# Down projection with an eighth ring slot, spaced ring loads and 35 new visits, and a last gate/up pair ordered product by product

## The chip, the cores and the metric

The kernel runs on one core of one Trainium2 chip. The core's engines work side by side, each on its own queue, in order: TensorE (PE) multiplies matrices and accumulates in PSUM; VectorE (DVE) and ScalarE (ACT) do elementwise work; GpSimd (POOL) does elementwise work and issues DMAs that accumulate; SyncE (SP) only issues DMAs. ACT issues DMAs too. An engine that waits for a semaphore holds up everything behind it on its queue. The metric is the device time of one execution in microseconds (us); less is better.

## The reference

One block of a hybrid model, in float32, for 512 tokens of width 2048. Only the last two steps matter here:

```python
D_FF = -((-8 * D_MODEL) // (3 * 256)) * 256        # 5632
...
    h = h + mixed @ w_out[l]
    v = rmsnorm(h, ffn_norm_w[l])
    h = h + (jax.nn.silu(v @ w_gate[l]) * (v @ w_up[l])) @ w_down[l]
return rmsnorm(h, final_norm_w)
```

Ahead of them stand a state-space mixer and a sparse attention; the change does not touch them.

## The kernel before

**Arithmetic.** Products keep float32 precision by splitting each operand into a high part (rounded to fp32r) and a low part (the rest); each product is three matmuls, high x high, high x low and low x high (L1252 to L1254, each with a moving operand of 256 columns). A 2 x 2 block product is done in Strassen's way with seven products M1 to M7 instead of eight. The tokens are split in two halves of 256 and the weights into quadrants "11", "12", "21", "22". The seven forms of the activations are made once ("V0", "VV", "T0" to "T3" for gate/up); the weight forms are made on the fly: "S1" is 21 + 22, "S3" is 21 + 11, and M6 and M3 take sums that DVE adds in place.

**Steps.** The feed-forward part is one list of steps (class `Step`, L1234). A step is one product over n rows (chunks of 128) of one weight block, 3 n matmuls. `run_step` (L1242) writes out, in order: `feed`, the step's `before`, `prep` of what lies two steps ahead, the matmuls (each chunk with a `tick` of the background tasks in `Sched`), and `after`, which takes the product out of PSUM. Each engine works through its own share of that list in order. `form` (L1205) makes the sums (DVE) and the high half (ACT); `prep` (L1221) makes the low half (DVE, L121) and frees the weight block. High halves are thus made up to three steps ahead and low halves up to two. They lie in R, 48 rows of 128 columns, which every step shares.

**Weight blocks.** `advance` (L1171) goes through the list `loads` in order and gives each block the free place that has been free longest: in Z (38 rows in the down projection, 48 before), E (8 rows), A[0:8] in gate/up, or A2 = A[70:76] in the down projection. Then it issues the load on SP; a block with `plus` gets an accumulating DMA on POOL on top; a block with `both` is the sum of two blocks, made by POOL.

**Gate/up.** 22 pairs u, each with two sides (0 gate, 1 up) of 7 products with n = 8: side 0 first, then side 1, in the order `SEQ`. A side has five blocks from DMA, two of them with an accumulating DMA. `gu_after` (L1419) combines the products in the tile CT, applies the norm and silu after side 0's M4 and multiplies the sides after side 1's M4. `g_forms` (L1457) then makes the seven forms of the result, spread over 14 ticks, in ST, and writes them to the DRAM tile g_d[u] (1.8 MB) on ACT's queue. A is one tile: HH is A[20:28], CT is A[28:44], ST is A[44:76], and the forms lie in A[44:72].

**Down projection.** The result is 8 column pairs j, each summed over the 22 chunks. It is done in 36 visits (j, n): visit v multiplies the next n chunks of column j, 7 products of 3 n matmuls, in the order `SEQ_D`. The accumulators H[j] lie in A[10 j : 10 j + 10] (H[7] in Z); `load_h` (L1555) puts the residual h into rows 1 to 4 of H[j] from DRAM, on ACT's queue. The activations come back through a ring of 7 slots, the places where the seven gate/up forms lay (chunks 0 to 6 of each; a form has 8). `feed` (L1541), at each step, issues at most one load, G[n], on ACT's queue, once the slot's last user lies at least two steps back; `done` holds the step after which a slot is free. In the last pair, slot i is free after the i-th product of side 1. `quad(..., s3_by_pool)` makes S3 with POOL in the first six visits and with an accumulating DMA behind them. `d_after` adds the products to H[j]; a column's last visit also runs `add_x` and `squares`. `d_end` ends the last visit, norms and writes out. `down_before` (L1695) loads H[v + 1] at product 1 of visit v and there makes A2 known.

## Time and profile before

| | us |
|---|---|
| runs of the kernel | 2313.32, 2312.17, 2308.17 (median 2312.17) |
| the profiled execution: its span, from the first to the last instruction | 2311.7 |
| PE busy in the span | 2196.5 (95%) |
| DVE busy | 1809.7 (78%) |
| ACT busy | 1091.2 (47%) |
| end of the last gate/up product | 1800.2 |
| last matmul of the down projection | 2294.1 |

A row of a group or timeline names the kernel's line, the engine, the operation, the tile written and the tiles read. In a wait row the arrow points to what ended the wait. A line can be that of a helper: L118 makes a high half, L121 a low half, L127 is an add. In the windows, "x" counts the instructions that begin or run in a window, and PEclk is the mean clock that PE was granted, where 1.00 is full. Tiles keep the name of the allocation: u, V and T are ring slots, A holds the accumulators and g's forms, Z and E hold weight blocks, R holds high and low halves.

### The profile page before, as it was taken

The numbers are of one execution on the slowest core, as the hardware profiler recorded it, in microseconds if no ns is written. First come the engines' busy times: TensorE is split into PE (matmuls) and PEld (weight loads), VectorE is DVE, ScalarE is ACT, GpSimd is POOL, SyncE is SP. The second block draws the span as 40 slices with busy tenths as digits, with TensorE's granted clock in tenths as the row PEclk, the third lists the DMA queues.
The fourth block names the chain that finished last, engine by engine and source line by source line (L and its number), as shares of the span: only waits on it lengthen the run. The fifth ranks groups of instructions, "written<-read, shape, count | busy, mean of one in ns | idle before, by whom it ended". The sixth has DMA issues, their size and how long they took to land. (4 is left out here: it accounts for less than half of the span.)

```text
span 2311.7 us, 39742 instructions
## 1 busy us (share of the span) xinstructions
PE 2196.5 (95%) x15376; PEld 2039.8 (88%) x15376; DVE 1809.7 (78%) x2921; ACT 1091.2 (47%) x1768; POOL 422.2 (18%) x435
## 2 busy tenths in 40 slices
PE   7999988989989989999999999999999698989997
PEld 5888877878878878999999999999999698989997
DVE  7799754768788857888888888888888697878786
ACT  4554433757676634544444444444444243333353
POOL 1011214132232134100000000000101121212122
PEclk9999989999999999999999999999999899999998
DMA  5222432221233366787878787887878857677776
GB/s 176 89 74 74 133 110 87 73 72 63 76 101 125 105 198 180 207 233 219 242 217 243 221 249 226 245 227 231 233 219 250 323 170 264 186 254 233 259 162 171
DMA packets 151469, 417.34 MB, mean 181 GB/s; under 512 B 16320, under 2 KB 21968, under 8 KB 151280
## 3 DMA queue, kind: packets, MB, share of 16 engines
q1 hardware_dynamic: 99264, 250.99, 31.5%
q0 software_dynamic: 25456, 76.78, 17.3%
q10 hardware_dynamic: 26560, 87.04, 10.5%
q8 instruction: 120, 1.97, 0.3%
q14 instruction: 69, 0.57, 0.1%
HBM read 353.67 MB, written 57.15 MB: 178 GB/s over the span
## 5 line engine op out<-in xcount | busy, mean ns | idle before, releaser
L118 ACT ACTIVATE R<-Z 128x1024 fp32r<-128x1024 f32 (+4 forms) x488 | 441.5, 922 | 573.0 <-DVE Z L127 320.6
L121 DVE TENSOR_TENSOR R<-Z,R 128x1024 fp32r<-128x1024 f32 (+4 forms) x381 | 392.3, 1035 | 28.5 <-ACT R L118 19.7
L241 PE MATMUL ps_g<-u,whi 128*128 128x512 f32 x720 | 301.1, 418 | 9.5 <-ACT whi L118 9.5
L242 PE MATMUL ps_g<-u,whi 128*128 128x512 f32 x720 | 284.3, 395 | 0.0
L243 PE MATMUL ps_g<-u,wlo 128*128 128x512 f32 x720 | 284.3, 397 | 0.0
L1252 PE MATMUL ps_g<-u,R 128*128 128x256 f32 (+1 forms) x834 | 250.5, 300 | 0.7 <-ACT R L118 0.7
L1253 PE MATMUL ps_g<-u,R 128*128 128x256 f32 (+1 forms) x834 | 249.7, 299 | 0.0
L1254 PE MATMUL ps_g<-u,R 128*128 128x256 f32 (+1 forms) x674 | 200.5, 298 | 0.1
L1252 PE MATMUL ps_t<-u,R 128*128 128x256 f32 x688 | 194.0, 282 | 0.0
L1253 PE MATMUL ps_t<-u,R 128*128 128x256 f32 x688 | 193.9, 282 | 0.0
L1252 PE MATMUL ps_s<-u,R 128*128 128x256 f32 x686 | 193.7, 282 | 0.0
L1253 PE MATMUL ps_s<-u,R 128*128 128x256 f32 x686 | 193.5, 282 | 0.0
L118 ACT ACTIVATE whi<-wraw 128x512 fp32r<-128x512 f32 x196 | 122.4, 626 | 145.2 <-PE ps_g L242 94.6
L121 DVE TENSOR_TENSOR wlo<-wraw,whi 128x512 fp32r<-128x512 f32 x196 | 145.9, 748 | 46.1 <-ACT whi L118 45.4
L241 PEld LDWEIGHTS ps_g<-u,whi 128*128 128x128 f32 x720 | 137.7, 191 | 33.1 <-ACT whi L118 11.4
L1252 PEld LDWEIGHTS ps_g<-u,R 128*128 128x128 f32 x834 | 158.3, 190 | 6.6 <-ACT R L118 0.9
L243 PEld LDWEIGHTS ps_g<-u,wlo 128*128 128x128 f32 x720 | 136.7, 190 | 30.7 <-DVE wlo L121 0.7
L1253 PEld LDWEIGHTS ps_g<-u,R 128*128 128x128 f32 x834 | 158.3, 190 | 5.9
L1254 PE MATMUL ps_s<-u,R 128*128 128x256 f32 x566 | 160.0, 283 | 0.6 <-DVE R L121 0.6
L242 PEld LDWEIGHTS ps_g<-u,whi 128*128 128x128 f32 x720 | 137.7, 191 | 19.7
L121 DVE TENSOR_TENSOR E<-Z,R 128x1024 fp32r<-128x1024 f32 x107 | 130.4, 1218 | 5.6 <-ACT R L118 5.6
L127 DVE TENSOR_TENSOR Z<-Z 128x1024 f32<-128x1024 f32 (+5 forms) x119 | 126.2, 1061 | 8.3 <-POOL Z L127 5.3
(449 smaller groups left out, 6464.3 us busy)
## 6 DMA issues: line engine op xcount, KB each, us to landing
Z<-in_w_gate SPq DMA_DIRECT2D x96, 512.0 KB, 5.3
Z<-in_w_up SPq DMA_DIRECT2D x94, 512.0 KB, 7.3
wraw<-in_w_in SPq DMA_DIRECT2D x164, 256.0 KB, 3.0
g_d<-A ACTq DMA_DIRECT2D x22, 1792.0 KB, 7.1
u<-g_d ACTq DMA_DIRECT2D x12, 1792.0 KB, 16.3
Z<-in_w_gate POOLq DMA_DIRECT2D x37, 512.0 KB, 7.4
Z<-in_w_up POOLq DMA_DIRECT2D x36, 512.0 KB, 5.6
Z<-in_w_down SPq DMA_DIRECT2D x52, 320.0 KB, 5.8
```

Source lines behind the costliest of these rows:

```text
L118: act.activation(dst, src, AF.Copy, scale=scale)
L121: eng.tensor_tensor(dst, src, f(hi), ALU.subtract)
L127: eng.tensor_tensor(o, a, b, ALU.add)
L241: pe.matmul(p, hi_t[i][:, j, :], ah, start=(k == 0), stop=False)
L242: pe.matmul(p, hi_t[i][:, j, :], al, start=False, stop=False)
L243: pe.matmul(p, lo_t[i][:, j, :], ah, start=False, stop=(k == u.nk - 1))
L1252: pe.matmul(q, h[:, k, :], ah, start=(k == 0), stop=False)
L1253: pe.matmul(q, h[:, k, :], al, start=False, stop=False)
L1254: pe.matmul(q, l[:, k, :], ah, start=False, stop=(k == s.blk.n - 1))
```

## The change

- The ring gets an eighth slot, made of chunk 7 of each of the seven forms. What goes there (G[7] and G[15]) is written to a DRAM tile g8_d of its own layout and loaded in seven pieces.
- Ring loads are at least 7 us apart by a planned clock (0.118 us a matmul), a piece one seventh of that.
- 35 visits instead of 36, small at the start (n = 2, 2, 3, 4, 5), mostly n = 6 behind that, and n = 4, 3, 3, 3, 5 at the end.
- The last pair goes product by product, gate and up in turn, in the order `SEQ_L`; both sides of a product share a PSUM bank, and `last_out` combines both at once; `last_gate` gates each quarter as soon as it is complete. S1 is summed by POOL, S3 by DVE as 11 (which by then holds 11 + 21 + 22) less 22. A slot is free after each two products. The last quarter is followed by g_forms.
- In the down projection, `prep` may go further ahead than two steps, up to 5 us of planned clock, where R has room.
- `load_h` comes at product 4 of visits 1 and 3 and at product 1 of the others; in visit 1 the write of g_d[21] is put ahead of it; A2 is made known in visit 3 at product 4.

```diff
-VISITS = [(0, 3), (1, 4), (2, 5), (3, 5), (4, 5), (5, 5), (6, 5), (7, 4), (0, 4), (7, 4), (4, 5), (1, 5), (6, 5), (2, 5),
-          (5, 5), (3, 6), (0, 4), (7, 4), (6, 5), (4, 6), (1, 5), (5, 6), (2, 6), (3, 5), (0, 5), (7, 4), (1, 4), (6, 4),
-          (7, 6), (6, 3), (3, 6), (5, 6), (1, 4), (2, 6), (4, 6), (0, 6)]
-GRING = 7
+VISITS = [(0, 2), (1, 2), (2, 3), (3, 4), (4, 5), (5, 6), (6, 6), (7, 6), (1, 6), (0, 5), (2, 6), (3, 6), (4, 6), (5, 6),
+          (6, 6), (7, 6), (0, 6), (1, 6), (2, 5), (3, 6), (4, 6), (6, 6), (5, 5), (7, 5), (0, 6), (1, 5), (2, 5), (3, 6),
+          (5, 5), (4, 5), (6, 4), (0, 3), (1, 3), (2, 3), (7, 5)]
+GRING = 8
+G_US, MM_US, AHEAD_US = 7.0, 0.118, 5.0
...
 BANK_D = {M1: (0, 0), M6: (1, 0), M2: (1, 1), M3: (2, 0), M7: (2, 1), M4: (3, 0), M5: (3, 1)}
-V_SLOT = [0, 1, 4, 5, 3, 2, 6]
+SEQ_L = [M1, M6, M5, M7, M4, M2, M3]
+V_SLOT = [V_OF[p] for p in SEQ_L]
...
-    loads, items, steps = [], [], []
+    loads, items, steps, clock = [], [], [], []
...
-    def form(upto):
+    def ready(i):
+        b, n = items[i][0], items[i][0].n
+        if hz.busy.count(False) < 14 or not hz.find(n, NR, range(0, NR - 5, 6)):
+            return False
+        advance()
+        return b.at is not None
+    def form(upto, must=None):
...
             i = nxt["form"]
+            if must is not None and i > must and not ready(i):
+                return
...
             assert b.at is not None, (i, fz.busy)
+            if b.src is None and b.both is None:
+                (x, y), = sums
+                dve.tensor_tensor(b.ap(), x.ap(), y.ap(), ALU.subtract)
+                x.read()
+                y.read()
+                sums = ()
...
-    def prep(upto):
-        form(upto)
+    def prep(upto, must):
+        form(must)
...
             i = nxt["item"]
-            form(i + 1)
+            form(i + 1, must + 1)
+            if nxt["form"] <= i or (i > must and not ready(i)):
+                return
...
             steps.append(self)
+            clock.append(clock[-1] + 3 * MM_US * steps[-2].blk.n if clock else 0.0)
...
             s.before()
-        prep(s.i + 2)
+        far = s.i + 2
+        while far + 1 < len(steps) and items[s.i][0].down and clock[far + 1] <= clock[s.i] + AHEAD_US:
+            far += 1
+        prep(far, s.i + 2)
...
         yield 6
-        nc.scalar.dma_start(g_d[u].rearrange("q p n -> p q n"), f(sg).rearrange("p v s t -> p (v s t)").rearrange("p (q n) -> p q n", q=4))
+        if u % GRING == GRING - 1:
+            nc.scalar.dma_start(g8_d[u // GRING].rearrange("v p n -> p v n"), f(sg).rearrange("p v s t -> p v (s t)"))
+        else:
+            nc.scalar.dma_start(g_d[u].rearrange("q p n -> p q n"),
+                                f(sg).rearrange("p v s t -> p (v s t)").rearrange("p (q n) -> p q n", q=4))
...
-                P2["slot"] = [P2["V0"], P2["VV"][:, 0], P2["T"][1], P2["T"][2], P2["T"][0], P2["VV"][:, 1], P2["T"][3]]
+                forms = [P2["V0"], P2["VV"][:, 0], P2["VV"][:, 1]] + [P2["T"][i] for i in range(4)]
+                P2["slot"] = [[forms[a][:, i] for i in range(7)] for a in V_SLOT]
+                P2["slot"].append([forms[a][:, 7] for a in V_SLOT])
+                P2["rows"] = [forms[a][:, 0:7] for a in V_SLOT]
...
     done = {}
-    for u in range(1, NP):
+    for u in range(1, NP - 1):
...
             af, bk = gu_after(u, side), banks()
-            for n, p in enumerate(SEQ):
+            for p in SEQ:
                 b, sums = qs[u, side]["form"][p]
-                s = Step(b, v_rhs(p), bk(p), after=af(p), sums=sums)
-                if (u, side) == (NP - 1, 1):
-                    done[V_SLOT.index(V_OF[p]) - GRING] = s.i
+                Step(b, v_rhs(p), bk(p), after=af(p), sums=sums)
+    def last_out(pr):
+        def ev(p):
+            ct = P2["CT"].rearrange("p (s q a) t -> p s q (a t)", s=2, q=4)
+            p = p.rearrange("p (s t) -> p s t", s=2)
+            p1, c11, c12, c21, c22 = P2["HH"][:, 2:4, :], *[ct[:, :, i, :] for i in range(4)]
+            if pr == M1:
+                act.activation(p1, p, AF.Copy)
+            elif pr == M6:
+                add(dve, c21, p, p1)
+            elif pr == M5:
+                dve.tensor_tensor(c12, c21, p, ALU.subtract)
+            elif pr == M7:
+                dve.tensor_tensor(c22, p, c12, ALU.subtract)
+                dve.tensor_tensor(c21, p, c21, ALU.subtract)
+                sch.add(last_gate(3))
+            elif pr == M2:
+                add(dve, c11, p, p1)
+                sch.add(last_gate(0))
+            elif pr == M3:
+                add(dve, c12, p, c12)
+                sch.add(last_gate(1))
+            else:
+                add(dve, c21, p, c21)
+                sch.add(last_gate(2))
+        return ev
+    def last_gate(i):
+        c = P2["CT"].rearrange("p (s q a) t -> p s q (a t)", s=2, q=4)[:, :, i, :]
+        mul(dve, c, c, rrow[:, None, (lo_h, hi_h)[i % 2]].to_broadcast([128, 2, 256]))
+        yield 3
+        act.activation(c[:, 0, :], c[:, 0, :], AF.Silu)
+        yield 3
+        mul(dve, c[:, 1, :], c[:, 1, :], c[:, 0, :])
+        if i == 1:
+            yield 2
+            yield from g_forms(NP - 1)
+    def pair_bank():
+        got = []
+        def get(side):
+            def g():
+                if not got:
+                    got.append(bank())
+                return got[0], got[0][:, 256 * side:256 * side + 256]
+            return g
+        return get
+    for side, w in ((0, w_gate), (1, w_up)):
+        q = qs[NP - 1, side] = quad(w[NP - 1], 0, 8, by_dma=False)
+        q["11"].reads, q["22"].reads = 4, 3
+        q["S3"] = Blk(8, 1)
+        q["form"][M7] = (q["S3"], [(q["11"], q["22"])])
+    for side, a in ((0, "11"), (1, "11"), (0, "21"), (0, "22"), (0, "S1"), (1, "21"), (1, "22"), (1, "S1"),
+                    (0, "S3"), (1, "S3"), (0, "12"), (1, "12")):
+        loads.append(qs[NP - 1, side][a])
+    for slot, p in enumerate(SEQ_L):
+        bk = pair_bank()
+        for side in range(2):
+            b, sums = qs[NP - 1, side]["form"][p]
+            s = Step(b, v_rhs(p), bk(side), after=last_out(p) if side else None, sums=sums)
+        done[slot - GRING] = s.i
+    done[-1] = s.i
...
+    pieces = [(n, a) for n in range(NP) for a in (range(7) if n % GRING == GRING - 1 else (None,))]
+    pace = {"at": 0.0, "n": 0}
...
-        n = len(G)
-        if n < NP and done.get(n - GRING, i) + 2 <= i:
-            if n == NP - 1:
-                sch.run_until(("g", n))
-            G[n] = P2["slot"][n % GRING][:, 0:7]
-            nc.scalar.dma_start(f(G[n]).rearrange("p v s t -> p (v s t)").rearrange("p (q n) -> p q n", q=4),
-                                g_d[n].rearrange("q p n -> p q n"))
+        if pace["n"] < len(pieces):
+            n, a = pieces[pace["n"]]
+            if done.get(n - GRING, i) + 2 <= i and clock[i] >= pace["at"]:
+                if n == NP - 1:
+                    sch.run_until(("g", n))
+                G[n] = P2["slot"][n % GRING]
+                if a is None:
+                    nc.scalar.dma_start(f(P2["rows"][n % GRING]).rearrange("p v s t -> p (v s t)").rearrange(
+                        "p (q n) -> p q n", q=4), g_d[n].rearrange("q p n -> p q n"))
+                else:
+                    nc.scalar.dma_start(f(G[n][a]).rearrange("p s t -> p (s t)"), g8_d[n // GRING, a])
+                pace["at"] = clock[i] + (G_US if a is None else G_US / 7)
+                pace["n"] += 1
...
         a = V_OF[p]
-        return lambda k: (G[lo_ + k][:, a, 0, :], G[lo_ + k][:, a, 1, :])
+        return lambda k: (G[lo_ + k][a][:, 0, :], G[lo_ + k][a][:, 1, :])
...
         def before():
-            if n == 1 and v:
+            if n == (4 if v in (1, 3) else 1) and v:
                 assert v < NJ - 2 or not any(fz.busy[NZ2:])
+                if v == 1:
+                    sch.run_until(("g", NP - 1))
                 load_h(v + 1)
-                P2["A2"] = P2["A"][:, 70:76, :]
+                if v == 3:
+                    P2["A2"] = P2["A"][:, 70:76, :]
...
             s = Step(blk, g_rhs(p, a), (lambda: (lambda t: (t, t[:, 0:256]))(bank())) if end else bk(p), after=af(p),
-                     before=down_before(v, n) if n < 2 and v < NJ - 1 else None, sums=sums)
+                     before=down_before(v, n) if v < NJ - 1 else None, sums=sums)
```

More of the change, by code (lines that the diff above doesn't have):

```diff
@@ L156, in body @@
     g_d = dram.tile([NP, 4, 128, 896], F32, name="g_d")
+    g8_d = dram.tile([NP // GRING, 7, 128, 512], F32, name="g8_d")
     pools = {}
@@ L1268, in pre_oa @@
         A = P2["A"] = wsp.tile([128, NA, 128], F32, name="A")
-        P2["T"] = {i: wsp.tile([128, 8, 2, 256], F32R, name=f"T{i}") for i in range(2)}
+        t01 = wsp.tile([128, 2, 8, 2, 256], F32R, name="T")
+        P2["T"] = {i: t01[:, i] for i in range(2)}
         P2["Z"] = wsp.tile([128, NZ, 128], F32, name="Z")
```

## The prediction

> **What bounds the kernel now.** I call T the end of the last gate/up product, 1800.2 us in this trace. The page comes first.
>
> ```profile
> span 2311.7 us, 39742 instructions
> ...
> PE 2196.5 (95%) x15376; PEld 2039.8 (88%) x15376; DVE 1809.7 (78%) x2921; ACT 1091.2 (47%) x1768; POOL 422.2 (18%) x435
> ...
> PEclk9999989999999999999999999999999899999998
> ```
>
> TensorE (PE) is busy 95% of the span, so only time in which PE stands still, or runs at a lower clock, can be won. The clock row counts tenths of full speed in 40 slices of 57.8 us, and from slice 31 on (1792 us, where the down projection begins) PE is weak in several places. So the next view is PE's waits from 1700 us on (total us, times, longest):
>
> ```profile
> PE ps_t L1254 <- DVE R L121: 12.0, 3, 11.2
> PE ps_t L1252 <- DMA V<-g_d: 7.0, 1, 7.0
> PE ps_t L1252 <- DMA T<-g_d: 6.9, 1, 6.9
> PE ps_g L1252 <- DMA T<-g_d: 6.0, 1, 6.0
> PE ps_g L1252 <- DMA V<-g_d: 4.8, 1, 4.8
> PE ps_m L1635 <- DVE acc L127: 2.3, 2, 1.5
> ```
>
> Four waits of 7.0, 6.9, 6.0 and 4.8 us are for a ring load (u, V and T are the ring's slots); one, of 11.2 within the first row, is for a VectorE (DVE) low half. Together 35.9 us. Then the stage in windows of 20 us (columns: PE, weight load, DVE, ScalarE (ACT), GpSimd (POOL), clock, DMA):
>
> ```profile
> 1800.00:1820.00 20.00, 13.08 (x88) 12.71 (x86) 16.27 (x25) 6.52 (x12) 3.38 (x2) 0.74 1.03 403
> 1820.00:1840.00 20.00, 9.20 (x76) 8.97 (x75) 6.37 (x12) 3.61 (x8) 3.06 (x2) 0.84 0.76 304
> 1840.00:1860.00 20.00, 19.54 (x152) 19.54 (x153) 19.05 (x24) 9.45 (x16) 7.23 (x4) 0.90 0.43 136
> ...
> 1920.00:1940.00 20.00, 14.39 (x120) 13.99 (x118) 14.55 (x24) 5.83 (x9) 2.76 (x2) 0.99 1.04 388
> 1940.00:1960.00 20.00, 19.50 (x143) 19.50 (x144) 13.67 (x19) 7.30 (x11) 3.94 (x3) 0.84 0.61 200
> ...
> 2040.00:2060.00 20.00, 13.00 (x92) 12.84 (x91) 10.23 (x14) 4.65 (x6) 2.70 (x2) 0.83 0.84 274
> ...
> 2080.00:2100.00 20.00, 20.00 (x172) 20.00 (x171) 15.05 (x22) 7.32 (x9) 2.66 (x2) 1.00 0.78 246
> ...
> 2160.00:2180.00 20.00, 15.18 (x130) 14.97 (x128) 14.79 (x25) 5.65 (x9) 2.69 (x2) 0.96 1.03 374
> 2180.00:2200.00 20.00, 19.27 (x140) 18.95 (x140) 12.12 (x20) 7.88 (x14) 3.71 (x3) 0.87 0.43 111
> 2200.00:2220.00 20.00, 19.59 (x158) 18.82 (x158) 17.14 (x27) 10.02 (x15) 4.41 (x4) 1.00 0.75 190
> ```
>
> 2080 to 2100 is the undisturbed case: 172 matmuls begin or run in 20 us, 0.118 us each, so 169.5 fit exactly. The disturbed windows fall short of that by 81.5, 93.5, 17.5 (two waits), 49.5, 26.5, 77.5, 39.5 and 29.5 matmuls: 415, or 49.0 us. Some 0.7 us of it are small waits near 2199, so the five stalls cost **48.3 us**: 35.9 of waiting and 12.4 of half clock behind each (the clock column: 0.74 to 0.87). The first costs 9.8, the second 12.9.
>
> Why the ring is late:
>
> ```profile
> 1789.05 1.14 ACTq L1548 DMA_DIRECT2D T<-g_d  x1
> ...
> 1807.41 0.58 PE L1252 MATMUL ps_t<-T,R 128*128 128x256 f32 x1 [6.92 <-DMA T<-g_d]
> ...
> 1812.36 1.07 ACTq L1476 DMA_DIRECT2D g_d<-A  x1
> ...
> 1835.67 1.53 POOL L127 TENSOR_TENSOR A<-Z 128x640 f32<-128x640 f32 x1 [31.10 <-DMA g_d<-A]
> ```
>
> Those are the timelines of ACT's queue, PE and POOL, each row with its start, its length and, in brackets, the idle time ahead of it; and this is how long the ring loads took, by their line:
>
> ```profile
> DMA to landing us min/median/max: 7.7/15.0/23.2
> ```
>
> G[2] is issued at 1789.05 and PE starts with it at 1807.41. By the loop's own steps (3 x n matmuls of 0.118 us) the loads G[2], G[7], G[14] and G[21] each go out 8.5 us before the visit that needs them; a ring load takes 7.7 to 23.2, median 15.0. Those are the four DMA stalls. The 11.2 us are another chain: the write of g_d[21], issued at 1812.36, reads A[44:72]; the zone A2 = A[70:76] is given out from visit 1, and a POOL sum placed there waits 31.1 us, until 1835.67. DVE, then PE, wait for that sum.
>
> **The change part by part.**
>
> *Ring.* Eight slots, earlier frees, bigger visits. The same arithmetic gives the issue and the need, from T. G[1]'s slot is free after the fourth of fourteen products, and the pace lets it go at the seventh: -22.7, needed at 0. G[3]: -5.7 and +17.3. G[10] replaces G[2], whose last visit is number 9 (0, 5): it goes in visit 10, +113.6, and visit 12 needs it at +141.2. G[21]: +328.9 and +351.9. The smallest lead of a whole load is 22.7 us, where it was 8.5. Of G[15]'s seven pieces the last has 12.4 and is one seventh as large. Loads 7 us apart move 1.835 MB / 7 = 262 GB/s; the windows above show up to 403. So all four DMA stalls go: 9.8 + (48.3 - 9.8 - 12.9) = 35.4 us. Had landings stayed at 23.2, a lead of 22.7 would lose 0.5. Six more ACT issues for each of two piecewise loads cost 0.37 each, beside an ACT that is busy 5 to 9 of 20 us: nothing. The g8_d write has rows of 2 KB instead of 3.5 KB; no row shows it, bounds 0 and +5 us of landing, both inside the lead: nothing.
>
> *A2 and h loads.* A2 is given out at visit 3, product 4, T+23 by PE's clock and later by what the opening loses, some 20 us behind the write's issue; the oldest free place is taken first, so the next block, one of visit 5, lands there. The 31.1 us wait has nothing urgent behind it any more: 12.9 us go. If the write took its 23 us again (1812.36 to 1835.67), SP's queue would stand about 3 us with 13 to spare: nothing. What is late next is the opening, below.
>
> *Last pair.* Per side, five loads and two accumulating DMAs become four loads; DVE gets one subtraction per side (1.14 a piece), POOL one sum. Seven evacuations of 512 columns replace ten of mixed width; four gates of 0.94 replace three passes of 1.1. A pair so far:
>
> ```profile
> 1720.90:1760.55 39.65, 39.65 (x337) 39.65 (x336) 32.85 (x38) 17.97 (x20) 2.59 (x3) 1.00 0.80 232
> ```
>
> DVE has 6.8 us to spare in 39.65. I add 2.3 for the subtractions, about 0.2 for the rest, and up to 6 if each POOL sum (unseen at 1024 wide; 768 takes 1.95, below) stops one DVE operation. Between 0 and +2 us; I take 0, as PE covers all but the top end.
>
> *The opening visits.* Here the change costs. DVE's rows:
>
> ```profile
> L121 DVE TENSOR_TENSOR A<-A 128x256 fp32r<-128x256 f32 x21 | 8.8, 418 | 0.0
> L121 DVE TENSOR_TENSOR R<-Z,R 128x384 fp32r<-128x384 f32 x14 | 7.6, 552 | 1.6 <-ACT R L118 1.3 <-issue 0.3
> L121 DVE TENSOR_TENSOR R<-Z,R 128x1024 fp32r<-128x1024 f32 x159 | 193.8, 1219 | 11.3 <-ACT R L118 8.5 <-PE ps_t L1254 1.4 <-PE ps_t L1253 1.3
> L127 DVE TENSOR_TENSOR A<-ps_s,A 128x512 f32<-128x512 f32 x68 | 46.8, 688 | 35.0 <-PE ps_s L1254 34.5
> L127 DVE TENSOR_TENSOR A<-ps_g,A 128x256 f32<-128x256 f32 x28 | 11.8, 420 | 15.1 <-PE ps_g L1254 14.2 <-ACT A L1589 0.8
> ...
> 1820.81 1.28 DVE L121 TENSOR_TENSOR R<-Z,R 128x512 fp32r<-128x512 f32 x2
> ...
> 1843.54 3.73 DVE L121 TENSOR_TENSOR R<-Z,R 128x640 fp32r<-128x640 f32 x2
> ...
> 1842.88 1.60 POOL L127 TENSOR_TENSOR E<-Z 128x640 f32<-128x640 f32 x1 [4.07 <-DVE R L121]
> 1844.56 2.03 POOL L127 TENSOR_TENSOR Z<-Z 128x640 f32<-128x640 f32 x1
> ```
>
> The first five are groups (last figures: busy us, mean ns, idle), the others timeline rows. Two operations of 0.68 take 1.28 together, so each costs its duration less 0.08: 0.34 at 256, 0.47 at 384, 0.60 at 512, 0.74 at 640 and 1.14 at 1024 columns. A visit has seven low halves and two sums of its width, and 2.8 us of evacuation (three of 512, three of 256, rounded). With n = 2: 9 x 0.34 + 2.8 = 5.9 us of DVE beside 7 x 2 x 3 x 0.118 = 5.0 us of PE. n = 3: 7.0 beside 7.4; n = 4: 8.2 beside 9.9. POOL's two sums stretch two low halves of 640 from 1.55 to 3.73 (they overlap in time), 2.2 a visit; scaled with n, 0.9 at n = 2. Ahead of that stand the last pair's evacuation (0.60), its last gate (0.60 and 0.34) and g_forms (0.60, 0.34 and 0.34 for the sums; 0.34, 0.60 and 1.14 for the low halves): 4.9. Through visit 1 DVE needs 4.9 + 2 x 6.8 - 0.7 (two low halves made ahead) = 17.8 us, PE 9.9: **7.9 late**. Visit 2 adds 0.9, visit 3 nothing. Before, the same tail lay in the shadow of the 6.9 us wait; now nothing covers it, and each visit behind has at most 2 us of slack to give, which PE cannot use to catch up.
>
> Then the h loads:
>
> ```profile
> DMA to landing us min/median/max: 3.2/4.0/17.1
> ```
>
> A[0:8] now holds a block of the last pair until its last product is formed, so H[0] goes out only behind G[3], about T-6, and is wanted at T+2.4 (evacuation, gate, three low halves). H[2] goes out at visit 1, product 4, right behind the write of g_d[21] on ACT's queue, and is wanted after the first product of visit 2, some 4 us later. Landing takes 3.2 to 17.1, more behind a ring transfer; DVE, in order, holds low halves behind that add. I take 0.5 and 2.7 us, bounds 0 and 8. Opening: 8.8 + 3.2 = **12 us**, bounds 3 (no block by POOL, evacuations off PE's path, h in time) and 20.
>
> The Trainium skill ("TensorE: Matmul & The Clock Gate", section "A second HAM failure mode: psum-queue depth-cycling") says that a PE that idles briefly between groups of matmuls, often enough, swings between half and full clock. The trace does not bear that out so far: 2200 to 2220 holds several waits of under 1 us, and its clock is 1.00.
>
> *Preparing up to 5 us ahead.* It needs 14 free rows of R's 48; four steps of n = 6 fill R. Bounds -2 and 0; I take 0.
>
> *The end.* Three visits of n = 3 that finish their column add 0.95 for add_x and 0.3 for the wider first evacuation, with one POOL sum 8.9 beside 7.4 us of PE: 4.5 us late over three. At visits 27 and 34 the fourth block is placed only 5.3 us before the sum that needs it is issued:
>
> ```profile
> Z<-in_w_down SPq DMA_DIRECT2D x36, 384.0 KB, 4.3
> ...
> L127 POOL TENSOR_TENSOR Z<-Z 128x768 f32<-128x768 f32 x4 | 7.8, 1948 | 31.4 <-DMA Z<-in_w_down 31.4
> ...
> 2293.94 0.28 PE L1254 MATMUL ps_s<-V,R 128*128 128x256 f32 x1
> ```
>
> 4.3 to land and 1.95 to add: about 1 us each, two steps being made ahead. Together 6.5. Against it: 1800.2 + 22 x 8 x 7 x 3 x 0.118 = 2236.5, the last matmul is at 2293.94, so 57.4 us were lost, of which 48.3 are the five stalls, about 2 the sum of squares inside the last visit, and some 7 small waits of the same kind, which the new visits replace. Net 0, bounds -3 and +5. The tail behind it, 17.6 us, stays.
>
> **Sum.** 2311.7 - 48.3 + 12 = 2275.4 for the profiled execution. Its time is its span, 2311.7; the median of the runs is 2312.17, 0.5 more. So **2276**, own range 2268 to 2284.
>
> **Rivals.**
>
> *The opening is nearly free* (17%): what DVE owes is made up by what is prepared ahead; 3 to 5 us instead of 12: 2267. For it: DVE idled just ahead of the old opening, as this row's bracket shows. Against: R was full of eight-row halves then, so nothing could be made ahead.
>
> ```profile
> 1799.83 0.69 DVE L127 TENSOR_TENSOR A<-ps_s,A 128x512 f32<-128x512 f32 x1 [3.34 <-PE ps_s L1254]
> ```
>
> *PE falls to half clock in the opening, or H[2] comes over 6 us late* (16%): at 0.236 us a matmul, visits 0 to 2 take 34.7 us instead of DVE's 26: 8 more, 2284; with a late H[2] too, 2292. That is what the page of the Trainium skill named above would make of it; the sentence about 2200 to 2220 is against it.
>
> *The ring stays late, so the change doesn't do what it says* (6%): loads are spaced by the planned clock, not by the real one, and bunch; two stalls of 9 remain: 2294. Against: leads of 22.7 and more.
>
> *Slower* (5%): seventeen visits of n = 6 instead of ten need five blocks each out of eight places. If the fourth block's landing and sum overrun its 8.5 to 12.7 us of lead by 2.5 in each, 42 us are lost: 2318. It decides at landings of about 9 us. Against: 2080 to 2100 runs two such visits in a row at 172 matmuls, with the same lead, and they land in 4.3.
>
> The rest (2%) is no change. A measurement of this kernel tells about 0.2% from none. My forecast has 54%. The range from 2264 to 2294 takes in the forecast and the first two rivals. Faster 0.93, same 0.02, slower 0.05.
>
> **What would show it.** No PE wait on g_d beyond 1 us. POOL without a wait on the g_d write. PE in short waits for DVE's R in T to T+25, about 12 us in all, clock mostly 1.00; DVE over 95% busy there but for an h_d wait. Last matmul about 36 us earlier. Wrong if: a g_d wait remains; PE is full right after T; or waits for w_down blocks appear in every n = 6 visit.

## The result, and the profile after

| | before | after |
|---|---|---|
| time, median of 4 runs each, us | 2311.26 (2308.17 to 2313.32) | 2289.84 (2289.28 to 2293.74) |
| span of the profiled execution, us | 2311.7 | 2292.0 |

The ratio is 0.991, 95% interval 0.9895 to 0.9925: 21.4 us less by the medians, 19.7 by the two spans. The profiled execution of after is the slowest of its four (2293.74, 1.7 above its span). The page of after:

```profile
PE 2197.8 (96%) x15376; PEld 2036.6 (89%) x15376; DVE 1810.1 (79%) x2910; ACT 1089.9 (48%) x1763; POOL 419.9 (18%) x431
...
PEclk9999989999999999999999999999999899999998
```

PE does the same 15,376 matmuls. The clock row is the same string as before: a slice of 57 us is too coarse for what has changed. PE's waits in after from 1700 us on (total us, times, longest):

```profile
PE ps_t L1278 <- DVE R L123: 9.0, 13, 1.9
PE ps_s L1278 <- DVE R L123: 5.3, 8, 1.3
PE ps_g L1278 <- DVE R L123: 3.8, 5, 1.2
```

No wait on g_d is left and none is longer than 1.9 us; where before had four ring waits and one of 11.2 us, there are 26 short ones for a VectorE (DVE) low half (L123 now). The same windows of 20 us as before show where they are:

```profile
1800.00:1820.00 20.00, 14.14 (x89) 12.91 (x88) 16.86 (x34) 7.90 (x20) 4.61 (x4) 0.85 0.74 286
1820.00:1840.00 20.00, 18.68 (x138) 18.14 (x138) 16.74 (x29) 8.53 (x16) 3.56 (x2) 0.90 1.01 375
1840.00:1860.00 20.00, 18.80 (x154) 18.19 (x153) 19.76 (x26) 6.43 (x10) 4.34 (x3) 1.00 0.77 270
1860.00:1880.00 20.00, 20.00 (x171) 20.00 (x170) 16.05 (x21) 9.92 (x14) 3.95 (x3) 1.00 0.71 220
2220.00:2240.00 20.00, 18.11 (x143) 16.96 (x142) 17.53 (x34) 10.71 (x22) 7.23 (x9) 1.00 0.83 187
2240.00:2260.00 20.00, 17.02 (x134) 15.86 (x133) 17.69 (x32) 9.85 (x20) 5.32 (x6) 1.00 0.64 134
```

At 169.5 matmuls for 20 us, the first three fall short by 80.5, 31.5 and 15.5 matmuls, 127.5 x 0.118 = 15.0 us; the fourth is full. The last two fall short by 62, 7.3 us: the end has got worse than it was.

For an exact balance I use the starts of the 11,472 matmuls of the list of steps in PE's timeline. All are there, so the first matmul of every visit is known. A visit of n chunks needs 21 n x 0.118 us; what it takes beyond is its **loss**. For all kernels of this study (us; "pair": the last gate/up pair, which needs 39.65; "sum": the pair's start to the last matmul; the last 8 visits are 27 to 34, or 28 to 35 where the old 36 visits, marked *, are used):

| kernel | pair | loss, visits 0 to 4 | middle | last 8 visits | sum | pair starts at |
|---|---|---|---|---|---|---|
| before * | 39.79 | 23.2 | 20.8 | 14.3 | 534.2 | 1759.8 |
| **after** | 41.58 | 15.9 | 4.4 | 15.7 | 513.7 | 1760.3 |
| a2_alone * | 39.79 | 16.0 | 16.3 | 13.5 | 521.7 | 1757.5 |
| old_visits * | 41.28 | 12.8 | 7.6 | 8.9 | 506.8 | 1758.6 |
| pair_by_side | 39.79 | 12.9 | 8.1 | 19.4 | 516.3 | 1761.8 |
| no_spacing | 45.56 | 22.5 | 3.4 | 14.9 | 522.5 | 1756.3 |
| no_ahead | 41.29 | 14.3 | 4.9 | 14.7 | 511.3 | 1755.5 |
| open_345 | 41.46 | 21.4 | 16.5 | 11.2 | 526.7 | 1760.1 |
| end_5 | 41.30 | 16.2 | 4.5 | 11.3 | 509.5 | 1761.4 |
| warm_fill | 41.26 | 18.7 | 7.3 | 13.0 | 516.3 | 1757.9 |
| h2_first | 41.46 | 17.1 | 4.4 | 13.3 | 512.3 | 1758.5 |
| squares_spread | 41.28 | 14.9 | 5.5 | 7.1 | 504.9 | 1758.0 |
| old_both * | 41.64 | 11.0 | 8.0 | 9.4 | 506.1 | 1759.2 |
| old_both_no_ahead * | 41.29 | 10.0 | 10.5 | 12.0 | 510.0 | 1756.8 |

The last column matters for reading all that follows: the pair starts between 1755.5 and 1761.8 us, although these kernels differ in next to nothing ahead of it. So one execution's time carries some 6 us that say nothing of the edit, and the sum is compared instead. The sum has a spread of its own: the code behind visit 4 is that of after in warm_fill, h2_first and pair_by_side, and there the middle and the last 8 visits together lose 20.3, 17.7 and 27.5 where after loses 20.1. So a sum can move by 2 to 3 us, in one case 7, in code that the edit doesn't touch, and a reading has to rest on the visits that it does touch. The opening is steadier: end_5 and squares_spread leave it as in after and lose 16.2 and 14.9 there for 15.9.

The balance of the change: the five stalls give 48.3 us, all of it. Against that stand, beyond before's other losses, 15.4 us in visits 0 to 4 (15.9, where before lost 0.5 beside its stalls), 1.9 in the middle, 8.8 in the last eight visits (15.7 - 6.9) and 1.8 in the pair. That is -48.3 + 27.9 = -20.4; the sums say 513.7 - 534.2 = -20.5. The start (0.45) and the tail (17.98 for 17.60) add 0.8, which gives the spans' 19.7.

### The profile page after: what moved, and what is told of

It reads as the page before. It is cut to its first block, busy times and chain, and to the rows that moved or that the text cites. A ratio compares the mean times of both kernels' runs of the same rounds, so it can differ in the third digit from the quotient of the medians.

```text
span 2292.0 us, 39682 instructions
## 1 busy us (share of the span) xinstructions
PE 2197.8 (96%) x15376; PEld 2036.6 (89%) x15376; DVE 1810.1 (79%) x2910; ACT 1089.9 (48%) x1763; POOL 419.9 (18%) x431
## 4 chain that ended last, share of the span: by engine, by line
PE 63%; DVE 11%; issue 3%; DMA 3%; ACT 2%; POOL 1%; DVEq 0%; ACTq 0%; POOLq 0%
PE ps_g L1278 7%; PE ps_g L1277 7%; PE ps_g L1276 7%; PE ps_t L1278 6%; PE ps_t L1276 5%; PE ps_t L1277 5%; PE ps_s L1278 5%; PE ps_s L1276 5%; PE ps_s L1277 5%; PE ps_g L244 2%; PE ps_g L245 2%; PE ps_g L246 2%; DVE R L123 2%; DMA Z<-in_w_down 1%; DVE A L129 1%
## 5 line engine op out<-in xcount | busy, mean ns | idle before, releaser
L120 ACT ACTIVATE R<-Z 128x1024 fp32r<-128x1024 f32 (+4 forms) x479 | 435.5, 927 | 557.2 <-DVE Z L129 321.2
L123 DVE TENSOR_TENSOR R<-Z,R 128x1024 fp32r<-128x1024 f32 (+5 forms) x373 | 392.8, 1059 | 33.9 <-ACT R L120 26.7
L1276 PE MATMUL ps_s<-u,R 128*128 128x256 f32 x699 | 196.3, 281 | 0.0
L1277 PE MATMUL ps_s<-u,R 128*128 128x256 f32 x699 | 195.9, 280 | 0.0
L1276 PE MATMUL ps_t<-u,R 128*128 128x256 f32 x673 | 189.7, 282 | 0.2 <-ACT R L120 0.2
L1277 PE MATMUL ps_t<-u,R 128*128 128x256 f32 x673 | 189.4, 281 | 0.0
L123 DVE TENSOR_TENSOR wlo<-wraw,whi 128x512 fp32r<-128x512 f32 x196 | 146.5, 751 | 46.1 <-ACT whi L120 45.4
L244 PEld LDWEIGHTS ps_g<-u,whi 128*128 128x128 f32 x720 | 138.2, 192 | 32.3 <-ACT whi L120 10.5
L1277 PEld LDWEIGHTS ps_g<-u,R 128*128 128x128 f32 x844 | 160.1, 190 | 5.9
L1276 PEld LDWEIGHTS ps_g<-u,R 128*128 128x128 f32 x844 | 159.7, 189 | 6.1 <-ACT R L120 0.4
L1278 PE MATMUL ps_s<-u,R 128*128 128x256 f32 x571 | 160.8, 282 | 1.6 <-DVE R L123 1.4
L1278 PEld LDWEIGHTS ps_g<-u,R 128*128 128x128 f32 x676 | 128.0, 189 | 6.9 <-DVE R L123 2.6
L123 DVE TENSOR_TENSOR E<-Z,R 128x1024 fp32r<-128x1024 f32 x106 | 129.0, 1217 | 5.6 <-ACT R L120 5.4
```

The costliest lines, as they stand in the source:

```text
L120: act.activation(dst, src, AF.Copy, scale=scale)
L123: eng.tensor_tensor(dst, src, f(hi), ALU.subtract)
L244: pe.matmul(p, hi_t[i][:, j, :], ah, start=(k == 0), stop=False)
L1276: pe.matmul(q, h[:, k, :], ah, start=(k == 0), stop=False)
L1277: pe.matmul(q, h[:, k, :], al, start=False, stop=False)
L1278: pe.matmul(q, l[:, k, :], ah, start=False, stop=(k == s.blk.n - 1))
```

## The experiments

Each kernel was run once with a profile, beside one run of the kernel before on the same chip. Three chips were used: the kernel before took 2309.77 on that of a2_alone, old_visits, no_spacing and pair_by_side, 2311.30 on that of no_ahead, open_345, warm_fill and end_5, and 2317.15 on that of the last four, h2_first, squares_spread, old_both and old_both_no_ahead.

### a2_alone: of the change only the later A2

The kernel before, with

```diff
                 load_h(v + 1)
-                P2["A2"] = P2["A"][:, 70:76, :]
+                if v >= 3:
+                    P2["A2"] = P2["A"][:, 70:76, :]
```

> The kernel before with one edit: A2 is made known from visit 3 on, not from visit 1. Theory (the sum placed in A2 waits for the write of g_d[21], and PE for that sum): visit 2's loss of 13.0 us goes to under 3, the four ring waits stay at 5 to 7 us each, and the time falls from 2311 by 9 to 13 us, to 2298 to 2302. Rival (A2 is only where the wait shows, and the weights of visits 2 and 3 are late for another reason): visit 2 still loses 8 or more, and the time falls by less than 5.

Measured: 2298.66 us. PE's waits from 1700 us on:

```profile
PE ps_t L1252 <- DMA V<-g_d: 7.6, 2, 7.1
PE ps_t L1252 <- DMA T<-g_d: 6.8, 1, 6.8
PE ps_t L1254 <- DVE R L121: 4.2, 6, 2.1
PE ps_g L1252 <- DMA V<-g_d: 3.7, 1, 3.7
PE ps_g L1252 <- DMA T<-g_d: 2.5, 1, 2.5
```

The row of 11.2 is gone, the longest wait for a low half is 2.1, and the ring waits stand, two of them shorter (3.7 and 2.5) than the expected 5 to 7. The cause is shown by visit 2: its loss falls from 13.0 to 5.2, so one moved line gives 7.8 us there, and 5.2 stay where under 3 were expected. DVE's view of 1790 to 1850 has a wait of 2.7 us for an h load, which the long wait had covered. The sum falls by 12.5 (534.2 to 521.7), close to the 12.9 that were written for A2, but by luck: 6.0 of it are visit 10, which waits for the ring (8.8 to 2.8), and why that wait got shorter I have not traced.

### old_visits: the change without its new visits

The kernel after, with the old list `VISITS`; ring, spacing, pair and A2 as in after.

> The changed kernel with the 36 visits of before; ring of eight, spacing and last pair stay. Leads by the planned clock are then 11.3 us at visits 10, 18 and 28, and 14.2 or more elsewhere. Theory (a spaced load lands in 8 to 10 us, and the small first and last visits are what DVE cannot follow): ring waits under 2 us each; the opening with n = 3, 4, 5 loses 5 to 10 us in place of 15.9, the end about 7 in place of 15.7; time 2275 to 2284. Rival (only the new visits give the leads that are needed): waits for g_d of 4 us or more with half clock behind them at two or three of the visits 10, 18, 28; time 2290 or more.

Measured: 2285.65 us, above the expected 2275 to 2284; the opening loses 12.8 where 5 to 10 were expected, the end 8.9 where about 7. The sum is 506.8. There is no wait on g_d here either. So the ring is cured without the new visits, by the eighth slot, the earlier frees and the spacing; what the eighth slot does alone was not run. In this pair of runs the **new visits cost 6.9 us** (513.7 - 506.8): 3.1 in visits 0 to 4, 6.8 at the end and 0.3 in the pair, less 3.2 in the middle (rounded).

### no_spacing: ring loads as soon as a slot is free

```diff
-G_US, MM_US, AHEAD_US = 7.0, 0.118, 5.0
+G_US, MM_US, AHEAD_US = 0.0, 0.118, 5.0
```

> The changed kernel with ring loads not spaced (0 in place of 7 us). Theory (the leads alone remove the ring waits; spacing only keeps loads from bunching): no wait of PE for g_d beyond 1 us; the h loads stand behind more ring loads, so the opening loses 16 to 19 us instead of 15.9; time 2289 to 2294. Rival (the spacing removes the waits): at least one wait for g_d of 4 us or more returns, time above 2296.

Measured: 2298.61 us, sum 522.5, worse than the theory's 2289 to 2294. It is in the rival's range of time, but without its mechanism: PE has no wait for g_d. The ring is not late, but its loads are in the way. ACT's timeline in visit 1 and PE's behind it:

```profile
1804.17 0.38 ACTq L1648 DMA_DIRECT2D u<-g_d  x1
...
1819.34 0.33 ACTq L1651 DMA_DIRECT2D u<-g_d  x1
1819.77 0.42 ACT L120 ACTIVATE R<-Z 128x256 fp32r<-128x256 f32 x1 [5.73 <-DMA u<-g_d]
```

```profile
1822.02 0.58 PE L1278 MATMUL ps_t<-V,R 128*128 128x256 f32 x1 [5.86 <-DVE R L123]
```

The trace has the semaphores: the issue at 1819.34, a piece of the eighth slot, waits for the semaphore that the ring load issued at 1804.17 still holds, and that load lands at 1819.32. ACT, in order, stood 5.73 us behind that issue, so a high half and a copy behind it were late, then DVE's low half, then PE by 5.86. The last pair, 45.56 us long, shows the same in ACT's timeline:

```profile
1775.13 0.37 ACTq L1648 DMA_DIRECT2D T<-g_d  x1
...
1791.92 0.37 ACTq L1648 DMA_DIRECT2D u<-g_d  x1
1792.41 1.06 ACT L120 ACTIVATE R<-Z 128x1024 fp32r<-128x1024 f32 x1 [9.23 <-PE ps_g L1278]
```

The bracket names PE, but the issue ahead of it begins at 1791.92, 0.02 us after the load issued at 1775.13 on the same semaphore has landed and before PE's product is done (1792.10): again a ring load's issue waits for an earlier ring load, and the high half behind it on ACT's queue waits with it (ACT idle for 9.23 us, not all of it lost). PE then stands 1.42 us for that high half. In after one ring load's issue ends such a wait too, at 1804.16, but ACT does not stand idle for it. The 7 us between loads are worth 8.8 us of the sum (4.0 in the pair and 6.6 in the opening, less 1.8 behind it), not by keeping the ring in time but by keeping its loads out of ACT's way.

### pair_by_side: the last pair as before

The kernel after, with `SEQ` in place of `SEQ_L` for the slots and the loop of the kernel before for the last pair:

```diff
-V_SLOT = [V_OF[p] for p in SEQ_L]
+V_SLOT = [V_OF[p] for p in SEQ]
...
-    for u in range(1, NP - 1):
+    for u in range(1, NP):
...
+                if (u, side) == (NP - 1, 1):
+                    done[n - GRING] = s.i
```

> The changed kernel with its last gate/up pair done as before, side by side; ring of eight, spacing and visits stay. Theory (the product order buys leads for the first ring loads, and costs 2 us in the pair itself): the pair takes 39.8 us instead of 41.6, but G[1] goes out only some 6 us ahead of the first visit, which waits 3 to 9 us for it and then runs at half clock; DVE makes up its work in that wait, so the opening loses 15 to 22 us in place of 15.9, and the time is 2288 to 2297. Rival (the order buys nothing): no ring wait at visit 0, time 2287 to 2288.

Measured: 2297.83 us, just above the theory's range, sum 516.3. The pair is back at 39.79, so its new form costs 1.8 us, by DVE: after has two PE waits for a low half in it. But the ring then waits once, 2.0 us in visit 0, less than expected, and visit 5 loses 4.1 that after doesn't. Pair and visits 0 to 5 together come out nearly even: 0.1 + 12.9 + 4.1 here, 1.9 + 15.9 + 0.1 in after. So this run shows no gain from the new order. The end loses 3.7 more than in after, far from the edit; I have not traced that.

### no_ahead: nothing prepared further ahead than two steps

```diff
-G_US, MM_US, AHEAD_US = 7.0, 0.118, 5.0
+G_US, MM_US, AHEAD_US = 7.0, 0.118, 0.0
```

> The changed kernel, but nothing is prepared more than two steps ahead (AHEAD_US = 0). Theory (the preparing ahead can do little, since R is full wherever visits are large): the time stays within 2 us of the changed kernel's 2290, the losses of the opening and of the last visits keep their place and size. Rival (the preparing ahead carries DVE over the small visits): the losses grow by 4 us or more, 2294 or later.

Measured: 2286.92 us, a little below the theory's range; against after's profiled execution 4.8 of it is the earlier start of the pair. The sum is 511.3, 2.4 below after. With the old visits it goes the other way (old_both_no_ahead, below, 3.9 above). No steady gain from preparing ahead is shown.

The run tells something else besides. In its visits 0 and 1 (1796.8 to 1815.5) PE has the same kind of short waits as in after, but the clock stays full and DVE has no wait for an h load:

```profile
1796.80:1806.80 10.00, 7.05 (x51) 6.10 (x50) 8.90 (x19) 4.53 (x11) 2.19 (x2) 1.00 1.03 400
1806.80:1816.80 10.00, 6.68 (x46) 5.50 (x45) 9.90 (x19) 3.21 (x9) 3.82 (x2) 1.00 0.62 210
```

These two visits lose 8.8 us where after loses 11.2. So DVE's own work costs some 8.8 there, and half clock and h load together at most 2.4 more; what is prepared ahead differs too, so this is a bound.

### open_345: larger first visits

`VISITS` begins (0, 3), (1, 3), (2, 4), (3, 5), (4, 6); visits 8, 18, 19, 20 and 24 are smaller by one chunk each.

> The changed kernel with larger first visits, (0, 3), (1, 3), (2, 4), (3, 5) in place of (0, 2), (1, 2), (2, 3), (3, 4), and the later visits smaller by as much; the end stays. Theory (the opening loses its 15.9 us because visits of n = 2 and 3 ask more of DVE than of PE, and because PE then falls to half clock): the loss of the first five visits falls from 15.9 to 8 to 10 us, the rest stays, 2283 to 2286. Rival (the opening waits for h loads and for the last pair's evacuation, whatever the visits' size): the loss stays at 13 to 16 us, 2288 to 2291.

Measured: 2306.29 us, sum 526.7. Both sides failed: the first visits lose 21.4, not 8 to 10, and not the rival's 13 to 16. DVE's timeline in visit 2 and ACT's queue ahead of it:

```profile
1835.41 0.42 DVE L127 TENSOR_TENSOR A<-ps_s,A 128x256 f32<-128x256 f32 x1 [5.45 <-DMA A<-h_d]
```

```profile
1818.34 0.38 ACTq L1502 DMA_DIRECT2D g_d<-A  x1
1818.82 0.46 ACTq L1646 DMA_DIRECT2D u<-g_d  x1
1821.44 0.34 ACTq L1658 DMA_DIRECT2D A<-h_d  x1
```

H[2]'s load stands behind the write of g_d[21] and a ring load, 1.8 MB each, and lands 13.9 us after its issue; DVE holds everything behind the add that wants it. The middle loses 16.5 as well: in visit 25 a low half waited 5.47 us for a high half and that for a w_down block. Whoever moves a visit moves the weight blocks' places and due times with it, so this run says that h loads hurt, but not what the sizes alone would do.

### warm_fill: PE kept busy in visits 0 and 1

```diff
             pe.matmul(q, l[:, k, :], ah, start=False, stop=(k == s.blk.n - 1))
+            if s.blk.down and s.blk.n == 2:
...
+                for _ in range(2):
+                    pe.matmul(P2["fill"][:, 0:256], h[:, k, :], ah, start=True, stop=True)
```

> The changed kernel with two matmuls of 256 columns into a spare bank behind each chunk of the visits of n = 2 (visits 0 and 1), whose result nobody reads: PE's work for these two visits rises from 9.9 to about 16.5 us, beside DVE's 13.6. If the half clock inside the opening costs 4.6 us beside DVE's own time: PE's clock stays at 1.00 in the opening, and the real matmuls of visits 2 to 4 lose less; the opening's loss against the changed kernel's products (with the fill's 6.6 us counted as loss) is 12 to 16 us, 2286 to 2290. If DVE alone binds (the half clock costs nothing, since PE would wait anyway): the loss grows to 16 to 20 us, 2290 to 2295.

Measured: 2293.64 us, sum 516.3. In after, windows of 2 us show the clock going down (columns as above); by the trace's clock records it is 0.50 from 1807.1 to 1810.5 and from 1817.3 to 1824.1:

```profile
1808.00:1810.00 2.00, 2.00 (x11) 2.00 (x11) 1.93 (x6) 0.00 (x0) 0.00 (x0) 0.50 1.02 398
...
1820.00:1822.00 2.00, 2.00 (x11) 2.00 (x11) 1.34 (x3) 0.00 (x0) 0.00 (x0) 0.50 1.04 335
```

With the fill visits 0 and 1 (1799.1 to 1819.6) run at full speed; the clock falls only at 1827.1, in visit 2:

```profile
1799.00:1809.00 10.00, 9.35 (x79) 9.14 (x78) 8.66 (x19) 3.47 (x10) 2.15 (x2) 1.00 1.04 399
1809.00:1819.00 10.00, 7.77 (x61) 7.15 (x60) 9.30 (x18) 4.03 (x9) 2.86 (x2) 1.00 0.46 165
```

Visits 0 and 1 then take 9.9 + 4.2 + 6.4 = 20.5 us, with 6.6 us of fill in them, where after takes 9.9 + 3.9 + 7.3 = 21.1 without. So 6.6 us of extra PE work cost nothing there. The fill gives back the half clock, at most 4.5 us of PE's time in these visits, so it still adds 2 us or more; PE was not the bound, DVE was. Visit 2 loses 5.7 instead of 2.0, as DVE waits 4.3 us for H[2] where it waited 2.05. The opening's 18.7 is in the range of "DVE alone binds", but 2.3 of the 2.8 us that it is worse are this h load. What the half clock costs by itself this run doesn't settle; no_ahead bounds it at 2.4 us in visits 0 and 1.

### h2_first: one load moved ahead of the write

```diff
         yield 6
+        if u == NP - 1:
+            load_h(2)
         if u % GRING == GRING - 1:
...
-                load_h(v + 1)
+                if v != 1:
+                    load_h(v + 1)
```

> The changed kernel with one DMA moved: the load of H[2] is issued right ahead of the write of g_d[21] instead of behind it and at visit 1's fifth product. If the order on ACT's queue makes H[2] late: DVE's wait for it in visit 2 (2.0 us in the changed kernel, 5.4 in open_345) goes, it lands in 4 to 5 us, and the loss of visits 0 to 4 falls from 15.9 to 13 to 14.5 us. Rival (DVE's own work binds and that wait only fills its slack): the loss stays within 0.7 us of 15.9.

Measured: 2290.93 us, sum 512.3. Visit 2 loses 1.0 instead of 2.0, visit 1 6.1 instead of 7.3; but visit 3 loses 4.9 where it lost 1.2, and the opening 17.1. DVE's timeline and ACT's queue say why:

```profile
1833.92 0.42 DVE L129 TENSOR_TENSOR A<-ps_t,A 128x256 f32<-128x256 f32 x1 [2.19 <-DMA A<-h_d]
```

```profile
1815.26 0.33 ACTq L1662 DMA_DIRECT2D A<-h_d  x1
1815.62 0.45 ACTq L1506 DMA_DIRECT2D g_d<-A  x1
1817.21 0.38 ACTq L1650 DMA_DIRECT2D u<-g_d  x1
1822.21 0.34 ACTq L1662 DMA_DIRECT2D A<-h_d  x1
```

H[2] is in time, but H[3], issued behind the same two transfers, lands 11.6 us after its issue and DVE waits 2.19 us for it in visit 3. The wait was moved by one column, not removed. The total lies outside what either side expected. Both h loads ahead of the write would be the next trial; it was not run.

### squares_spread: the column's squares one by one

```diff
-                    squares(j)
+                    sch.add(squares(j))
...
+            yield 3
             act.activation(o, out_rows(j)[:, c, :], AF.Square)
...
-        weigh(j, slice(0, 512))
+        for c in range(2):
+            yield 3
+            a_hi(out_rows(j)[:, c, :], out_rows(j)[:, c, :], scale=col(C_LN + 2 * j + c))
```

> The changed kernel with the sums of squares of a finished column (two passes of Square and two that weigh it, 2.5 us of ACT in a row) given to ACT one by one, three chunks of the product apart, instead of all at once ahead of the next high halves. If ACT's order costs the end: DVE's waits for ACT R in visits 31 to 34 (0.7 to 1.7 us each) go, and the loss of these visits falls from 12.8 to 8 to 10 us. Rival (DVE's own work binds there): the loss stays at 12 to 13.5 us.

Measured: 2282.38 us, sum 504.9, the lowest of all. Visit 30, (6, 4), finishes column 6; in after, this is ACT, and then DVE, in visit 31, (0, 3), behind it:

```profile
2228.40 1.15 ACT L1677 ACTIVATE E<-A 128x512 f32<-128x512 f32 x2 [0.34 <-DVE A L1704]
2229.46 1.32 ACT L120 ACTIVATE A<-A,colc 128x512 f32<-128x512 f32 x2
2230.68 2.17 ACT L120 ACTIVATE R<-Z 128x384 fp32r<-128x384 f32 x5
```

```profile
2231.22 0.56 DVE L123 TENSOR_TENSOR R<-Z,R 128x384 fp32r<-128x384 f32 x1 [1.32 <-ACT R L120]
```

ACT does two squares and two weighing passes in a row, 2.5 us, and the high halves queue behind them; DVE, short of time at n = 3, stands 1.32 us. DVE's waits for a high half near the end: first after (2220 to 2265 us), then squares_spread (2210 to 2255, which ends 11 us earlier):

```profile
DVE R L123 <- ACT R L120: 6.7, 6, 1.7
```

```profile
DVE R L123 <- ACT R L120: 0.3, 1, 0.3
```

Visits 31 to 34 lose 7.0 instead of 12.8, below the expected 8 to 10. The wait itself is no accident of one execution: in after, h2_first, warm_fill and pair_by_side DVE stands 0.7 to 1.3 us for a high half once in each of the visits 28 to 33, and in squares_spread in none of them. In visits 28 and 29 of after (n = 5) that wait costs 0.0 and 0.4 us, at n = 3 it shows. Its price is less sure than 5.8: in the six other runs that end with the same visits and the squares in a row, visits 31 to 34 lose between 10 and 17 us, so 3 us are shown against the best of them and 5.8 against after. Visit 27 loses nothing instead of 1.9, but so it does in h2_first, so that isn't the squares' doing. In after ACT waits there for an accumulating DMA, DVE stands 1.76 us behind that, and PE 1.44 us later in the visit:

```profile
2180.80 3.58 ACT L120 ACTIVATE R<-Z 128x768 fp32r<-128x768 f32 x5 [1.98 <-DMA Z<-in_w_down]
```

### end_5: the finishing visits larger

`VISITS` has (0, 4), (1, 3), (2, 3) as visits 24 to 26 and ends (0, 5), (1, 5), (2, 5), (7, 5).

> The changed kernel with the end alone altered: visits 24 to 26 are (0, 4), (1, 3), (2, 3), and the three that finish columns 0 to 2 are (0, 5), (1, 5), (2, 5) in place of (0, 3), (1, 3), (2, 3). Theory (visits of n = 3 that finish a column are bound by DVE): the loss of visits 31 to 34 falls from 12.8 us to 5 to 7, visits 25 and 26 take up to 2 us more, 2283 to 2287. Rival (the finishing sums and the last visit's sum of squares cost it at any size): it stays at 11 to 13 us, 2289 to 2292.

Measured: 2290.29 us, above the expected range, with the pair 1.1 us later than in after; the sum is 509.5, 4.2 below. Visits 31 to 34 lose 8.1 instead of 12.8, a little above the expected 5 to 7. DVE's wait for a high half is still there, 1.0 to 1.2 us in each of the visits 28 to 33, so larger visits give DVE slack for the same wait. What visits 32 and 33 still lose (2.7 and 1.7) goes with a wait that after doesn't have there: DVE stands 2.77 and 2.15 us for a POOL sum.

### old_both and old_both_no_ahead

old_visits with the edits of h2_first and squares_spread, and that with AHEAD_US = 0.

> old_visits with both edits, H[2]'s load ahead and the squares spread. If both mechanisms hold beside the old visits: from the last pair's start to the last matmul 506.8 us become 500 to 504, the span 2277 to 2281 if what lies ahead of the pair takes as long. If they don't: 506 to 508.

Measured: 2285.28 us, sum 506.1, only 0.7 below old_visits and within what was expected if the mechanisms don't hold there. The last eight visits lose 9.4 (8.9 without): there the squares fall into visits of n = 6 and 4 but for one, where DVE can wait for ACT without PE noticing; that is argued from after's visits 28 and 29 and was not tested with the old visits. Visit 2 falls from 4.8 to 0, but visits 3 and 4 take 3.1 of it back, as in h2_first.

> old_both without preparing further ahead than two steps. Theory (preparing ahead is worth nothing): from the last pair's start to the last matmul within 1.5 us of old_both. Rival (the changed kernel's 513.7 against no_ahead's 511.3 was its price): 2 us or more below old_both.

Measured: 2286.52 us, sum 510.0, 3.9 above old_both: outside the theory's 1.5, and against the rival's sign. With after's visits the same edit gave 2.4 the other way. The difference lies in visits 19 and 28 (6.3 and 3.6 for 2.5 and 1.5); I haven't followed it further.

**A better version.** squares_spread has the lowest sum and, at 2282.38 us in one execution, lies below all four runs of after (2289.28 to 2293.74), though on a chip where the kernel before was slower than elsewhere (2317.15). It was run only once. Of the 8.8 us between the two sums 5.8 lie in visits 31 to 34, which the edit touches, and 1.9 in visit 27, which is not its doing; an interval is not known.

## Why the prediction was right or wrong

- **The forecast**, 2276, lies 13.8 us below the median of 2289.84. That median is outside the forecast's own 2268 to 2284. It is inside 2264 to 2294 only because that range takes in two rivals, neither of which happened as written. The direction and the place of the gain were right; the sum was too good by 16.6 us of span (2275.4 against 2292.0).
- **The five stalls: right.** All 48.3 us went. The two causes named are shown apart: the A2 zone by a2_alone (7.8 of the 12.9 in visit 2; that its whole sum moved by 12.5 is luck), the ring by old_visits and no_spacing, which have no g_d wait. The share of the eighth slot among the ring's three measures stays open. The landing times fell as well: 7.6, 9.5 and 15.0 us (minimum, median, maximum) for the whole ring loads of after, by their line, where before had 7.7, 15.0 and 23.2:

```profile
DMA to landing us min/median/max: 7.6/9.5/15.0
```

- **The opening, 12 us: mis-sized; 15.9, of which 15.4 are new.** DVE waited 1.16 us for H[0] and 2.05 for H[2]. That this makes the forecast's 3.2 is luck, as 0.5 and 2.7 were written, and not all of it reaches PE: without the 2.05, in h2_first, visit 2 loses 1.0 less. The other part, DVE's own lateness, was put at 8.8; what is left of the loss is 12.7. The excess lies in visits 0 and 1 (8.4 forecast, 11.2 measured) and in 2 to 4 (3.6 and 4.7). DVE's work through visit 1 was sized well at 17.8 us: the windows behind T, where it ends (DVE is the third busy time), hold 17.4 in 20.

```profile
1801.90:1811.90 10.00, 8.12 (x52) 7.51 (x50) 8.46 (x19) 3.60 (x11) 2.00 (x2) 0.83 1.04 398
1811.90:1821.90 10.00, 6.01 (x32) 5.40 (x31) 8.97 (x17) 3.88 (x9) 2.61 (x2) 0.77 0.44 161
```

  What I had left out is that DVE isn't fed without a break. Its timeline has, besides the two h loads, 0.99 us for a product that PE delivers late, at half clock. In no_ahead, without half clock and h loads, visits 0 and 1 lose 8.8, near the 7.9 that were written for DVE alone:

```profile
1805.32 0.42 DVE L129 TENSOR_TENSOR A<-ps_t,A 128x256 f32<-128x256 f32 x1 [1.16 <-DMA A<-h_d]
...
1820.66 1.02 DVE L129 TENSOR_TENSOR A<-ps_t,A 128x512 f32<-128x512 f32 x2 [0.99 <-PE ps_t L1278]
...
1827.32 0.42 DVE L129 TENSOR_TENSOR A<-ps_s,A 128x256 f32<-128x256 f32 x1 [2.05 <-DMA A<-h_d]
```

- **The half clock.** I set it aside because 2200 to 2220 of before held micro-waits at clock 1.00. In after the clock went to 0.50 twice, with no PE wait above 1.9 us. The Trainium skill ("TensorE: Matmul & The Clock Gate", section "HAM oscillation — how this bites in real kernels") warns of idle gaps above about 3.4 us as what slows PE; this trace shows the half clock without one, at 1.9. It fits the rule weighed in the prediction, from the Trainium skill's section "A second HAM failure mode: psum-queue depth-cycling", but how often is often enough stays open: no_ahead has eight waits of 0.3 to 1.6 us in visits 0 and 1 and keeps its clock at 1.00. So this half of the rival came true, and its price of 8 us did not appear: by no_ahead it is at most 2.4 in visits 0 and 1, and warm_fill shows DVE as the bound. Its other half, H[2] over 6 us late, did not come (2.05).
- **The last pair, 0: at the upper bound.** 1.8 us of the written 0 to +2. pair_by_side gets them back and loses them again in visits 0 to 5.
- **Preparing ahead, 0: not refuted**, with contrary signs of 2.4 and 3.9 us in the two pairs of runs.
- **The end, 0: the failed step.** I wrote 6.5 us of new waits against "some 7 small waits of the same kind, which the new visits replace". The end got 8.8 us worse, and both halves failed. The new waits were mis-sized: visits 31 to 33 lose 7.3 (4.5 written), visit 27 1.9 (1 written) and the last visit 5.5 (1 and 2 for its sum of squares written). And the small waits were not replaced: the middle loses 4.4 where before lost 2.6 beside its stalls. The cause of the first is that DVE and POOL were counted for the finishing visits, and ACT was not: its 2.5 us of squares and weighing stand ahead of the next high halves. With most of them in visits of n = 4 and 6 this is covered, at n = 3 it isn't (squares_spread gets 5.8 us back against after, old_both none). Visit 27 was late by a weight block, as written, but by its accumulating DMA and not by a POOL sum. The other 1 us or so stays open. (A slip beside it: 1800.2 + 436.1 is 2236.3 and not 2236.5, so 57.6 us were lost; nothing hangs on the 0.2.)
- **The rest:** 1.9 us in the middle (old_visits has more there) and 0.8 of start and tail. 1.8 + 3.4 + 8.8 + 1.9 + 0.8 = 16.7, the error of the forecast.
- **The rivals:** the ring that stays late did not come, and the w_down blocks that overrun in each visit of n = 6 did not either; a late block shows in visit 27 (1.9), while visits 5 to 8, 10 to 12 and 14 to 18, nearly all of n = 6, lose 0.1 us or nothing each. "The opening is nearly free" is refuted by 15.9.

## What to carry to other kernels

Once a long stall is gone, the steps in its shadow show: size them on every engine that they use, also the one that is half idle on average, because an in-order queue delays what stands behind it for as long as its burst lasts. A small tile saves waiting for data, but takes away the slack that hides such bursts. Before small loads (the h loads here) are put on a queue, look at what stands ahead of them, and where a queue both computes and issues DMAs, ask what each issue itself waits for. Compare edits by a stretch of the trace that holds the edit alone when the rest of the program moves by several us from one execution to the next.

## What was not expected of the hardware

That a POOL sum holds up DVE was in the prediction, as 2.2 us for two sums; one case shows how closely. In after's opening, POOL's and DVE's timelines and the group of that DVE operation:

```profile
1814.97 1.34 POOL L129 TENSOR_TENSOR Z<-Z,E 128x512 f32<-128x512 f32 x1
```

```profile
1815.10 2.30 DVE L123 TENSOR_TENSOR A<-A 128x1024 fp32r<-128x1024 f32 x1
```

```profile
L123 DVE TENSOR_TENSOR A<-A 128x1024 fp32r<-128x1024 f32 x22 | 27.9, 1266 | 0.1
```

The other 21 of the group, none of which meets a POOL sum, take (27.9 - 2.3) / 21 = 1.22 us; this one took 1.08 more, and POOL's sum ended 1.21 after it had begun. The Trainium skill ("SBUF — State Buffer", section "SBUF: two separate sides") says that the two share a port pair that one of them holds for a whole instruction while the other blocks; the numbers agree. What was not expected is that ACT can stand for 5.73 us behind a DMA issue that waits for an earlier ring load to land (no_spacing), which delays its arithmetic, not only its DMAs.
